# Pair 0 with seven block products in the first layer's two out projections

## The chip, the core and the metric

The kernel runs on one core of a Trainium2 chip. The metric is the device time of one execution in microseconds (us); before the change the median of three runs is 959.14 us (958.94 to 959.21). Five engines work side by side, each through its own instructions in the order in which the program lists them: TensorE (PE in the profile; its weight loads are shown apart as PEld), VectorE (DVE), ScalarE (ACT), GpSimd (POOL) and SyncE (SP), which here issues the DMA transfers. An instruction that needs another engine's result waits for a semaphore, and everything behind it on its engine waits with it.

## The reference, cut to what matters

A decoder trunk of two layers over 256 tokens with 1024 channels. Layer 0 is a short convolution between two half-step FFNs, layer 1 is sparse attention between two such FFNs:

```python
def swiglu_ffn(x, w_in, w_out):
    gate, up = jnp.split(x @ w_in, 2, axis=-1)
    return (jax.nn.silu(gate) * up) @ w_out
...
        h = h + 0.5 * swiglu_ffn(rmsnorm(h, ffn1_norm[i]), ffn1_w_in[i], ffn1_w_out[i])
        hn = rmsnorm(h, mix_norm[i])
        if i < N_A_LAYERS:
            h = h + short_conv_mixer(hn, conv_w_in[i], conv_w[i], conv_w_out[i])
...
        h = h + 0.5 * swiglu_ffn(rmsnorm(h, ffn2_norm[i]), ffn2_w_in[i], ffn2_w_out[i])
```

`w_in` is 1024 x 5632, `w_out` is 2816 x 1024. Everything is float32. The kernel gets near to that precision by splitting each float32 operand into a rounded high part and a remainder, the low part, and multiplying high by high, low by high and high by low.

## The kernel before

**The stages.** For layer 0: FFN 1 (its `ffn_in`, then its out projection `inner_pairs`), the convolution, FFN 2 (the same two steps), then keys and values, the attention layer, and the last FFN. The change touches the two FFNs of layer 0; the program of each is nearly the same.

**`ffn_in`** makes the 2816 hidden channels in 22 tiles of 128, numbered 0 to 21 here. For one tile PE runs 32 matmuls (L487) into a PSUM tile named `mm`. There are two `mm` buffers in use in turn, so a tile's first matmul waits until the tile two before it has been read out. The reading is done in `total`: ACT copies one half out (L505) and DVE adds the other half to it (L506). Then follow, on both engines in turn, the scaling by the norm (L517), silu (L530), gate times up (L531) and the split of the result for the next projection (`Pairs.add`; L499, L500, L554, L555).

**The weights** come through one stream, `W`. SP loads a chunk into a staging buffer (`ws`, of which there are three, or one of a few other places, `W.other`); then for each unit of 1024 columns ACT writes the high part (`high`; L250, or L173 for units of an out projection) and DVE the low part (`low`; L278 or L184) into buffers `wh` and `wl`, six of each. `weave` and `pump` put these two instructions between those of the tile's evacuation, so ACT and DVE carry them in the gaps of the tiles, and some units of the next stage are made while the last tiles of `ffn_in` still run.

**The out projection** takes the hidden tiles two by two: 11 pairs, 0 to 10, with 256 hidden channels each. Tokens, channels and outputs are cut in two, so that a pair is a 2 x 2 by 2 x 2 block product. A pair in `PLAIN0` or `PLAIN1` (the two FFNs) takes eight block products; any other takes seven (a Strassen-like scheme, products 1 to 7) from sums of the operands. Each block product is three matmuls of 128 x 512 (L821). The eight products add up into eight PSUM banks over all pairs: four in banks named `a`, four in two double banks named `mm` (`t57`, which holds products 5 and 7, and `t68`, with 6 and 8). `t57` lies on the buffer that tile 21 of `ffn_in` used, `t68` on that of tile 20. Later PE work in `inner_pairs` turns the sums back into the layout of `h`.

A pair's weights have the units (pair, kind): (p, 0) and (p, 4) for a plain pair; (p, 0), (p, 1), (p, 2) and (p, 3) for a pair with seven products. Kind 1 has half the size and a home of its own (`second_home`). Between kinds 1 and 2 DVE forms sums of the staged weights in place (`sums`, L179: three instructions). On the activation side a plain pair splits both hidden tiles whole; a pair with seven products forms four sums of 128 x 128 (L585) and splits those (L554, L555) when its second tile comes.

`Blocks.product` lists a pair's matmuls in an order that is written out: for a plain pair 0 products 2 and 8, then 4 and 3; for a pair 0 with seven, products 1 and 2, then 6 and 7 together, 5, 3 and 4. `S.ahead` sets how many units may be made before `ffn_in` is over.

Of the kernel before, what the change touches and what calls it, by code (L numbers as in the profile page):

```python
# [10 lines left out]
F32R = mybir.dt.float32r  # L11
# [5 lines left out]
P = 128  # L17
# [22 lines left out]
NBUF = 6  # L40
# [22 lines left out]
def trunk(ctx, tc, A, out):  # L63
# [11 lines left out]
    def mk(shape, tag, bufs, dt=F32, pool=None):  # L75
        uid[0] += 1
        return (pool or sb).tile(list(shape), dt, tag=tag, name=f"{tag}_{uid[0]}", bufs=bufs)
# [10 lines left out]
    def act(shape=(P, 512), dt=F32R):  # L88
        return mk(shape, "act", 22, dt)

    def t2(shape=(P, 512), dt=F32):
        return mk(shape, "t2", 7, dt)
# [19 lines left out]
    class Stream:  # L112
# [9 lines left out]
        def add(self, src, lo=0, hi=None, joint=0):  # L122


            hi = src.shape[1] if hi is None else hi
            while lo < hi:
                n = min(CHUNK, hi - lo)
                for u in range(max(n // 1024, 1)):
                    self.where.append((len(self.src), u, joint))
                self.src.append(src[:, lo:lo + n])  # L130
                lo += n

        def add_pairs(self, src, homes, plain):

            n, c0 = src.shape[1] // CHUNK, len(self.src)
            S = Section()
            S.home, S.plain, S.c0, S.at, S.pair, S.steps = homes, plain, c0, len(self.where), {}, []
            for p in range(n):
                self.paired.add(len(self.src))
                self.src.append(src[:, p * CHUNK:(p + 1) * CHUNK])  # L140
            todo = ([(0, 0), (0, 4)] if 0 in plain else [(0, 0), (0, 1), (0, 2), (0, 3)]) + ([] if 1 in plain else [(1, 0), (1, 1)])
            S.ahead = len(self.where) + len(todo)
            for p in range(n):
                now = [(p + 2, 0), (p + 2, 1)] if p + 2 < n and p + 2 not in plain else []
                if p + 1 < n:
                    last = [(p + 1, 2), (p + 1, 3)]
                    now = [(p + 1, 0), (p + 1, 4)] + now if p + 1 in plain else now + last if p else last + now
                todo += now
                S.steps.append(len(now))
            S.ahead += 3  # L150
            for _ in range(3):
                S.steps[next(p for p in range(n) if S.steps[p])] -= 1
            for p, kind in todo:
                if kind == 1:
                    self.spare.add(len(self.where))
                self.where.append((c0 + p, (S, p, kind), "pair"))
            S.n, S.reach = len(todo), 3
            return S

        def pair_high(self, c, S, p, kind):  # L160
            self.load(c + 2 if p == 0 and kind < 2 else c)
            st = self.stage[c]
            if kind == 1:
                src, (h, l) = st[:, 3:], S.home(p)
            else:
                src = st[:, 2:] if kind in (2, 4) else st[:, :2]
                h, l = mk([P, 2, 512], "wh", NBUF, F32R), None
            if kind == 2 and p > 1:
                self.sums(st)
                for x in range(2):  # L170
                    ac.copy(h[:, x], src[:, x])
            else:
                ac.copy(h, src)  # L173
            self.half.append((src, h, l, st, S, p, kind))

        def sums(self, st):

            for a, b, d, n in ((1, 2, 1, 2), (3, 3, 1, 1), (0, 0, 3, 1)):
                ve.tensor_tensor(out=st[:, a:a + n], in0=st[:, b:b + n], in1=st[:, d:d + n], op=ALU.subtract)  # L179

        def pair_low(self, src, h, l, st, S, p, kind):
            if l is None:
                l = mk([P, 2, 512], "wl", NBUF, F32R)
            ve.tensor_tensor(out=l, in0=src, in1=h.bitcast(F32), op=ALU.subtract)  # L184
            S.pair[p, kind] = h, l
            self.units.append(None)
            if kind == 1 and p < 2:
                self.sums(st)
            if kind in (3, 4):
                self.load(min(S.c0 + p + S.reach, S.c0 + NP + 1))  # L190
# [120 lines left out]

    NP = NF // 2
    PLAIN = (0, 2, 4, 6, 9, 10)
    PLAIN0 = (0, 2, 5, 8, 9, 10)
    PLAIN1 = (0, 2, 5, 8, 9, 10)
    TURNS = (3, 5, 7, 9)

    def second_home(p):
        tag, bufs = ("pr", 6) if p == 0 else ("t2", 7) if p == 1 else ("xs", 8)
        return [mk([P, 1, 512], tag, bufs, F32R) for _ in range(2)]  # L320

    W = Stream()
    W1AT = (13, 13)
    W.add(A["ffn1_w_in"][0])
    SEC0 = W.add_pairs(A["ffn1_w_pairs"], second_home, PLAIN0)
    W.other.update({SEC0.c0 + p: (1, "kt", 0, "ws", "ws")[p % 5] for p in range(NP)})
    SEC0.reach = 4
    W.spare.add(len(W.where) + 2)
    W.add(A["conv_w_in"])
    W.add(A["conv_w_out"])  # L330
    W.add(A["ffn2_w_in"][0])
    SEC1 = W.add_pairs(A["ffn2_w_pairs0"], second_home, PLAIN1)
    W.other.update({SEC1.c0 + p: (1, 0, "ws", "ws", "ws")[p % 5] for p in range(NP)})
    SEC1.reach = 4
    W.spare.add(len(W.where) + 2)
# [14 lines left out]
    W.other.update({n0 + f: (0, 1, "kt", "ws")[f % 4] if f < 14 else ("kt", 0, 1)[(f - 14) % 3] for f in range(4, NF + NP) if f != NF + 2})  # L350
    W.other = {c: at for c, at in W.other.items() if at != "ws"}
    SEC2 = W.add_pairs(A["ffn2_w_pairs1"], second_home, PLAIN)


# [5 lines left out]
    h = [kt8[:, c, :T] for c in range(ND)]  # L360
# [34 lines left out]
    def new_xs():  # L395
        return [mk([P, 512], "xs", 8, F32R) for _ in range(8)]
# [150 lines left out]
    class Pairs:  # L547
# [15 lines left out]
        def add(self, s):  # L563
            self.f.append(s)
            p, odd = divmod(len(self.f) - 1, 2)
            if p in self.plain:
                if not odd:
                    self.left.append([])
                self.left[p] += self.whole(s)
                return  # L570
            if not odd:
                if self.both is None:
                    self.both = act()
                    a = self.both[:, :T]
                else:
                    a, self.both = self.both[:, T:], None
                self.left.append([self.parts(a[:, :P], a[:, P:], s[:, :P])])
                return
            x1, x2 = self.f[-2:]
            a12, a22 = self.whole(x2)  # L580
            self.left[p] += [a12, None, a22]
            t = t2([P, 4, P])
            for o, a, b, op in ((t[:, 0], x1[:, P:], x2[:, P:], ALU.add), (t[:, 1], t[:, 0], x1[:, :P], ALU.subtract),
                                (t[:, 2], x1[:, :P], x1[:, P:], ALU.subtract), (t[:, 3], x2[:, :P], t[:, 1], ALU.subtract)):
                ve.tensor_tensor(out=o, in0=a, in1=b, op=op)  # L585
            h, l = [x.rearrange("p (a m) -> p a m", m=P) for x in self.homes(self.n)]
            self.parts(h, l, t)
            s1, s2, s3, s4 = [(h[:, i], l[:, i]) for i in range(4)]
            self.n += 1
            self.left[p][2] = s4  # L590
            self.left[p] += [s1, s2, s3]
# [109 lines left out]
    xs = new_xs()  # L701
# [89 lines left out]
        return r  # L791

    def first_home(n):
        return [mk([P, 512], "pr", 6, F32R) if x < 6 else mk([P, 512], "hm", 5, F32R) for x in (2 * n, 2 * n + 1)]

    X = {}

# [32 lines left out]
    def inner_pairs(S, left, rows, make, hold, first):  # L830
# [12 lines left out]
        def plus(name, n, tt):  # L843
            add(s[name], n, s[name], tt)
# [12 lines left out]
        def firsts():  # L857
            s["s1"], s["u2"], s["u3"] = t2(), t2(), t2()
            ac.copy(s["s1"], m[1])
            add(s["u2"], 6, s["s1"])  # L860
            add(s["u3"], 7, s["u2"])
# [58 lines left out]

    W.cap = SEC0.ahead
    hid = Pairs(first_home, PLAIN0)
    ffn_in(xs, nm, sums=first_tiles(), rms=first_rms, hid=hid, bg=rows_bg)

# [63 lines left out]

    inner_pairs(SEC0, hid.left, X["rows"], conv_norm, t2, conv_first)
    del hid  # L990
    xs, nm = X["xs"], X["nm"]
# [21 lines left out]
    xs = new_xs()  # L1013
# [29 lines left out]

    W.cap = SEC1.ahead
    hid = Pairs(first_home, PLAIN1)
    ffn_in(xs, nm, pre=lambda: list(tab), bg=second_bg, hid=hid)

# [101 lines left out]

    inner_pairs(SEC1, hid.left, X["rows"], lambda: nm, lambda: mk([P, 512], "pr", 6), kv_first)  # L1150
    del hid
    xs = new_xs()
# [167 lines left out]
    xs = new_xs()  # L1320
# [320 lines left out]
    xs = new_xs()  # L1641
# [189 lines left out]
```

## Time and profile before

| what | value |
|---|---|
| runs | 958.94, 959.14, 959.21 us |
| profiled execution, its own time | 959.4 us |
| its span, first to last instruction | 957.5 us |
| mean granted TensorE clock | 1.000 |
| PE busy / DVE busy / ACT busy | 99% / 84% / 64% of the span |
| `ffn_in` of FFN 1, tiles 3 to 21 | 24.78 to 130.37 us |
| matmuls of its out projection begin | 130.37 us |
| the same in FFN 2 | 400.79 us |

The rows of the timeline give the start in us from the first instruction, the duration in us, the engine, the line, the operation, the tiles written and read, shapes and a count of merged instructions; in brackets the idle time of the engine ahead of it and what ended it. The chain of waits follows the last instruction back to what released it. Ends of matmuls are modelled (one of 128 x 512 shows 0.39 us while its successor starts 0.23 us after it), so the distance from start to start is what counts on PE; on DVE an instruction may start some 0.08 us before the one ahead of it ends, and there too the distance between starts is used.

### The profile page before, as it was taken

Reading aid. Unit: us, or ns where it says so; the run is one execution under the profiler, and the core shown is the slowest. Engines: PE = TensorE matmul, PEld = TensorE weight load, DVE = VectorE, ACT = ScalarE, POOL = GpSimd, SP = SyncE. Lnnn points to the kernel's source line nnn. Section 1 sums busy time; section 2 is a strip of 40 time slices with the busy share of each in tenths; the row PEclk is TensorE's granted clock in tenths of the full one; section 3 lists DMA queues with packets and bytes.
Section 4 is the critical chain, followed back from the end, with each engine's and each line's share of the span. In section 5 each row is a group of like instructions: output and inputs, shape, how many; then the busy total and the mean of one; then the engine's idle time right before and its main releaser. Section 6 shows DMA issues by size and latency. Waiting matters only on the chain.

```text
span 957.5 us, 14525 instructions
## 1 busy us (share of the span) xinstructions
PE 951.2 (99%) x5431; PEld 827.5 (86%) x5431; DVE 803.5 (84%) x1332; ACT 613.0 (64%) x1048; POOL 144.5 (15%) x231
## 2 busy tenths in 40 slices
PE   8999999999999999999999999999999999999998
PEld 7888888888888888888888898889987888888887
DVE  6898899898898888898969787866588888878996
ACT  7666565565556666565857777754579656656553
POOL 1000000024460000000021042001337350000002
PEclk9999999999999999999999999999999999999999
DMA  8665844364546567553636867554520363467452
GB/s 300 230 216 186 307 149 160 132 208 164 201 138 243 197 208 254 175 196 132 220 132 188 265 212 259 177 201 163 215 89 2 132 221 143 166 222 247 148 179 84
DMA packets 42150, 178.58 MB, mean 187 GB/s; under 512 B 3777, under 2 KB 7505, under 8 KB 27105
## 3 DMA queue, kind: packets, MB, share of 16 engines
q1 hardware_dynamic: 42080, 177.67, 54.1%
q8 instruction: 42, 0.69, 0.3%
q14 instruction: 28, 0.22, 0.1%
HBM read 175.52 MB, written 1.08 MB: 184 GB/s over the span
## 4 chain that ended last, share of the span: by engine, by line
PE 97%; DVE 1%; ACT 1%; DMA 1%; SPq 0%; issue 0%
PE mm L487 55%; PE a L487 13%; PE a L821 12%; PE mm L821 5%; PE a L1124 1%; PE mm L1477 1%; PE a L1547 1%; PE mm L728 1%; PE a L1522 1%; PE a L767 1%; DMA base<-in_first_dram 1%; DVE pr L1485 0%; PE a L1217 0%; PE a L1063 0%; PE a L1065 0%; PE a L1064 0%
## 5 line engine op out<-in xcount | busy, mean ns | idle before, releaser
L487 PE MATMUL mm<-xs,wh 128*128 128x512 f32 x1480 | 349.2, 390 | 0.0
L487 PEld LDWEIGHTS mm<-xs,wh 128*128 128x128 f32 x1480 | 273.6, 188 | 54.8 <-DVE xs L410 0.5
L278 DVE TENSOR_TENSOR wl<-ws,wh 128x1024 fp32r<-128x1024 f32 x217 | 271.1, 1258 | 28.2 <-ACT wh L250 18.4
L250 ACT CAST wh<-ws 128x1024 fp32r<-128x1024 f32 x217 | 224.6, 1045 | 14.9 <-PE a L487 7.3
L487 PEld LDWEIGHTS mm<-xs,wl 128*128 128x128 f32 x1480 | 185.2, 192 | 4.2
L487 PE MATMUL mm<-xs,wl 128*128 128x256 f32 x1480 | 187.3, 283 | 0.0
L506 DVE TENSOR_TENSOR t<-mm,t 128x512 f32<-128x512 f32 x95 | 65.2, 686 | 46.2 <-ACT t L505 45.5
L505 ACT COPY t<-mm 128x512 f32<-128x512 f32 x95 | 55.4, 583 | 52.5 <-PE mm L487 51.8
L821 PE MATMUL a<-wh,act 128*128 128x512 f32 x306 | 81.7, 390 | 0.0
L821 PEld LDWEIGHTS a<-wh,act 128*128 128x128 f32 x306 | 57.3, 188 | 11.8
L530 ACT ACTIVATE t<-t 128x256 f32<-128x256 f32 x88 | 36.8, 418 | 45.9 <-DVE t L517 45.7
L487 PE MATMUL a<-act,wh 128*128 128x512 f32 x256 | 60.0, 390 | 0.0
L487 PEld LDWEIGHTS a<-act,wh 128*128 128x128 f32 x256 | 47.5, 188 | 9.4
L499 ACT CAST act<-t 128x256 fp32r<-128x256 f32 x81 | 33.0, 407 | 29.1 <-DVE t L944 18.5
L406 ACT ACTIVATE xs<-base 128x256 fp32r<-128x256 f32 x32 | 16.1, 508 | 50.1 <-DVE base L637 35.2
L517 DVE TENSOR_TENSOR t<-t,R 128x256 f32<-128x256 f32 (+1 forms) x88 | 45.0, 511 | 2.6
L821 PE MATMUL a<-wl,act 128*128 128x512 f32 x153 | 46.9, 389 | 0.0
L184 DVE TENSOR_TENSOR wl<-base,wh 128x1024 fp32r<-128x1024 f32 x38 | 45.6, 1221 | 0.1
L531 DVE TENSOR_TENSOR t<-t,t 128x256 f32<-128x256 f32 x88 | 37.0, 420 | 4.1 <-ACT t L530 4.1
L500 DVE TENSOR_TENSOR act<-t,act 128x256 fp32r<-128x256 f32 x81 | 35.5, 438 | 4.7 <-ACT act L499 4.7
L173 ACT CAST wh<-base 128x1024 fp32r<-128x1024 f32 x33 | 33.6, 1045 | 4.8 <-DVE base L179 3.0
L821 PEld LDWEIGHTS a<-wl,act 128*128 128x128 f32 x153 | 28.7, 188 | 6.0
(361 smaller groups left out, 1405.5 us busy)
## 6 DMA issues: line engine op xcount, KB each, us to landing
ws<-in_ffn_w_in_dram SPq DMA_DIRECT2D x69, 1024.0 KB, 4.9
base<-in_ffn_w_pairs_dram SPq DMA_DIRECT2D x32, 512.0 KB, 4.8
ws<-in_conv_w_in_dram SPq DMA_DIRECT2D x12, 1024.0 KB, 4.8
ws<-in_ffn_w_pairs_dram SPq DMA_DIRECT2D x22, 512.0 KB, 4.9
ws<-in_ffn_w_out_dram SPq DMA_DIRECT2D x11, 1024.0 KB, 4.8
base<-in_ffn_w_in_dram SPq DMA_DIRECT2D x11, 1024.0 KB, 5.3
kt<-in_ffn_w_pairs_dram SPq DMA_DIRECT2D x12, 512.0 KB, 4.5
ws<-in_w_kv_dram SPq DMA_DIRECT2D x6, 1024.0 KB, 4.9
```

What stands on the lines that cost most here:

```text
L173: ac.copy(h, src)
L184: ve.tensor_tensor(out=l, in0=src, in1=h.bitcast(F32), op=ALU.subtract)
L250: ac.copy(h, src)
L278: ve.tensor_tensor(out=l, in0=src, in1=h.bitcast(F32), op=ALU.subtract)
L487: pe.matmul(o if x == 0 else o[:, :T], u[x][:, q * P:(q + 1) * P], rhs if x == 0 else rhs[:, :T], start=start, stop=stop, skip_group_check ...
L500: ve.tensor_tensor(out=dst[:, T:], in0=src, in1=dst[:, :T].bitcast(F32), op=ALU.subtract)
L505: ac.copy(r, o[:, :, T:])
L506: ve.tensor_tensor(out=r, in0=o[:, :, :T], in1=r, op=ALU.add)
L517: ve.tensor_tensor(out=r, in0=r, in1=R[:, None, :].to_broadcast([P, n, T]), op=ALU.mult)
L530: ac.activation(s, r[:, 0], AF.Silu)
L531: ve.tensor_tensor(out=s, in0=s, in1=r[:, 1], op=ALU.mult)
L821: pe.matmul(self.m[n], x, w, start=(c == 0), stop=(c == 3 * self.total[n] - 1), skip_group_check=True)
```

## The change

It has four parts.

1. `PLAIN0` and `PLAIN1` lose pair 0, so that six of the eleven pairs take seven products in both FFNs of layer 0. `PLAIN`, of the last FFN, keeps it.
2. The first unit (0, 0) of such a section no longer takes a buffer of `wh` and one of `wl`: it has its own place, the tile `kt` (`own`). The home of (0, 1) is in `act` instead of `pr`. Since `kt` is taken, the staging places of the first section become those of the second, (kt8, kt8, ws, ws, ws).
3. Pair 0's sums of the weights come at its kind 1, those of pair 1 now at kind 2 like the later ones. The half unit (p + 2, 1) is made after (p + 1, 2) and (p + 1, 3) instead of ahead of them.
4. The sums of pair 0's activations are formed when the sixth hidden tile (tile 5) is added, not when its second is. The new method is `sums`.

```diff
-        def add_pairs(self, src, homes, plain):
+        def add_pairs(self, src, homes, plain, own=()):
...
-                    now = [(p + 1, 0), (p + 1, 4)] + now if p + 1 in plain else now + last if p else last + now
+                    now = [(p + 1, 0), (p + 1, 4)] + now if p + 1 in plain else now[:1] + last + now[1:] if p else last + now
...
-                if kind == 1:
+                if kind == 1 or (p, kind) in own:
                     self.spare.add(len(self.where))
...
-                h, l = mk([P, 2, 512], "wh", NBUF, F32R), None
-            if kind == 2 and p > 1:
+                if (p, kind) in S.own:
+                    t = mk([P, 4, 512], "kt", 1, F32R)
+                    h, l = t[:, :2], t[:, 2:]
+                else:
+                    h, l = mk([P, 2, 512], "wh", NBUF, F32R), None
+            if kind == 2 and p > (0 in S.plain):
...
-            if kind == 1 and p < 2:
+            if kind == 1 and p <= (0 in S.plain):
                 self.sums(st)
...
-    PLAIN0 = (0, 2, 5, 8, 9, 10)
-    PLAIN1 = (0, 2, 5, 8, 9, 10)
+    PLAIN0 = (2, 5, 8, 9, 10)
+    PLAIN1 = (2, 5, 8, 9, 10)
...
-        tag, bufs = ("pr", 6) if p == 0 else ("t2", 7) if p == 1 else ("xs", 8)
+        tag, bufs = ("act", 22) if p == 0 else ("t2", 7) if p == 1 else ("xs", 8)
...
-    SEC0 = W.add_pairs(A["ffn1_w_pairs"], second_home, PLAIN0)
-    W.other.update({SEC0.c0 + p: (1, "kt", 0, "ws", "ws")[p % 5] for p in range(NP)})
+    SEC0 = W.add_pairs(A["ffn1_w_pairs"], second_home, PLAIN0, [(0, 0)])
+    W.other.update({SEC0.c0 + p: (1, 0, "ws", "ws", "ws")[p % 5] for p in range(NP)})
...
+                if len(self.f) == 6 and 0 not in self.plain:
+                    self.sums(0)
                 return
...
-            x1, x2 = self.f[-2:]
-            a12, a22 = self.whole(x2)
+            a12, a22 = self.whole(s)
             self.left[p] += [a12, None, a22]
+            if p:
+                self.sums(p)
+
+        def sums(self, p):
+            x1, x2 = self.f[2 * p:2 * p + 2]
             t = t2([P, 4, P])
```

**The end of `ffn_in` on DVE.** This is DVE in FFN 1 between tile 18 and tile 19 of `ffn_in` (`act_212` and `act_214` hold tile 18's split, `mm_222` and `mm_227` are tile 19). Before:

```order
L500 TENSOR_TENSOR act_212_1196<-t1_209_1187,act_212_1196 128x256
L506 TENSOR_TENSOR t2_214_1232<-mm_213_1199,t2_214_1232 128x512
L517 TENSOR_TENSOR t2_214_1232<-t2_214_1232,R_47_310 128x256
L278 TENSOR_TENSOR wl_216_1238<-ws_202_1139,wh_215_1236 128x1024
L531 TENSOR_TENSOR t1_217_1240<-t1_217_1240,t2_214_1232 128x256
L278 TENSOR_TENSOR wl_220_1248<-ws_202_1139,wh_218_1243 128x1024
L500 TENSOR_TENSOR act_221_1250<-t1_217_1240,act_221_1250 128x256
L506 TENSOR_TENSOR t2_223_1286<-mm_222_1253,t2_223_1286 128x512
L517 TENSOR_TENSOR t2_223_1286<-t2_223_1286,R_47_310 128x256
L184 TENSOR_TENSOR wl_225_1294<-base_70,wh_224_1292 128x1024
```

and now, from the split of the same tile 18:

```order
L505 TENSOR_TENSOR act_222_1257<-t1_219_1248,act_222_1257 128x256
L189 TENSOR_TENSOR kt_224_1263<-base_70,kt_224_1263 128x1024
L189 TENSOR_TENSOR act_226_1267<-base_70,act_225_1266 128x512
L184 TENSOR_TENSOR base_70<-base_70 128x2x512
L184 TENSOR_TENSOR base_70<-base_70 128x512 x2
L511 TENSOR_TENSOR t2_228_1306<-mm_227_1273,t2_228_1306 128x512
L522 TENSOR_TENSOR t2_228_1306<-t2_228_1306,R_47_310 128x256
L189 TENSOR_TENSOR wl_230_1312<-base_70,wh_229_1310 128x1024
```

Between tile 18's split and tile 19's reading stand five instructions that were not there: the low parts of (0, 0) and (0, 1) and the three weight sums of pair 0. In the tile's own places for units stand (0, 2) and (0, 3) where (0, 0) and (0, 4) stood. In FFN 2 the same five stand at the same place.

**The start of the out projection on PE.** These are the first rows on PE behind tile 21 in FFN 1, with the semaphores that each waits for. `act_59`, `act_61` and `pr` are pair 0's activations. Before (`mm_255` is `t68`; `t57` is not written by pair 0, its first row is pair 1's):

```order
L821 MATMUL a_251_1424<-wh_224_1292,act_61_346 128x512 x2
L821 MATMUL a_251_1424<-wl_225_1294,act_59_339 128x512 [waits DVE_49]
L821 MATMUL a_251_1424<-wl_225_1294,act_61_346 128x512
L821 MATMUL mm_255_1428<-wh_227_1299,act_59_339 128x512 [waits DVE_49]
L821 MATMUL mm_255_1428<-wh_227_1299,act_59_339 128x512
L821 MATMUL mm_255_1428<-wh_227_1299,act_61_346 128x512 x2
```

and now (`mm_260` is `t68`, `mm_259` is `t57`):

```order
L832 MATMUL a_255_1442<-kt_224_1263,act_59_339 128x512 x2
L832 MATMUL a_256_1443<-kt_224_1263,act_61_346 128x512 x2
L832 MATMUL a_255_1442<-kt_224_1263,act_59_339 128x512
L832 MATMUL a_256_1443<-kt_224_1263,act_61_346 128x512
L832 MATMUL mm_260_1447<-wh_229_1310,pr_94_528 128x512 [waits DVE_49]
L832 MATMUL mm_260_1447<-wh_229_1310,pr_95_529 128x512
L832 MATMUL mm_259_1446<-wh_229_1310,pr_94_528 128x512 [waits DVE_49]
L832 MATMUL mm_259_1446<-wh_229_1310,pr_95_529 128x512
```

The first write into `t57` moves from the 34th matmul of the section (pair 1's tenth) to the ninth. In the built program that row waits for DVE's addition of tile 21, the last reader of the buffer; the first write into `t68` waits for that of tile 20.

**The sixth tile on DVE.** This is DVE in FFN 1 behind the split of the sixth hidden tile (`act_92`, `act_93`). Before, the reading of the next tile follows at once:

```order
L500 TENSOR_TENSOR act_93_521<-t1_89_512,act_93_521 128x256
L506 TENSOR_TENSOR t2_95_557<-mm_94_524,t2_95_557 128x512
L517 TENSOR_TENSOR t2_95_557<-t2_95_557,R_47_310 128x256
L278 TENSOR_TENSOR wl_97_563<-ws_77_448,wh_96_561 128x1024
L531 TENSOR_TENSOR t1_98_565<-t1_98_565,t2_95_557 128x256
```

and now:

```order
L505 TENSOR_TENSOR act_92_520<-t1_88_511,act_92_520 128x256
L596 TENSOR_TENSOR t2_93_523<-t1_55_330,t1_60_343 128x128
L596 TENSOR_TENSOR t2_93_523<-t2_93_523,t1_55_330 128x128
L596 TENSOR_TENSOR t2_93_523<-t1_55_330 128x128
L596 TENSOR_TENSOR t2_93_523<-t1_60_343,t2_93_523 128x128
L560 TENSOR_TENSOR pr_95_529<-t2_93_523,pr_94_528 128x512
L511 TENSOR_TENSOR t2_97_565<-mm_96_532,t2_97_565 128x512
```

Five instructions now stand ahead of tile 6's reading, the last of them behind ACT's copy of the sums.

More of the change, by code (lines that the diff above doesn't have):

```diff
@@ L137, in add_pairs @@
             S.home, S.plain, S.c0, S.at, S.pair, S.steps = homes, plain, c0, len(self.where), {}, []
+            S.own = own
             for p in range(n):
@@ L331, in trunk @@
     W.add(A["ffn2_w_in"][0])
-    SEC1 = W.add_pairs(A["ffn2_w_pairs0"], second_home, PLAIN1)
+    SEC1 = W.add_pairs(A["ffn2_w_pairs0"], second_home, PLAIN1, [(0, 0)])
     W.other.update({SEC1.c0 + p: (1, 0, "ws", "ws", "ws")[p % 5] for p in range(NP)})
@@ L793, in first_home @@
     def first_home(n):
-        return [mk([P, 512], "pr", 6, F32R) if x < 6 else mk([P, 512], "hm", 5, F32R) for x in (2 * n, 2 * n + 1)]
+        return [mk([P, 512], "pr", 6, F32R) if x < 6 else mk([P, 512], "hm", 5, F32R) if x < 11 else act() for x in (2 * n, 2 * n + 1)]
     X = {}
```

## The prediction

> **What bounds the kernel now.** The page comes first: shares of busy time, and the chain of work that ended last.
>
> ```profile
> span 957.5 us, 14525 instructions
> PE 951.2 (99%) x5431; PEld 827.5 (86%) x5431; DVE 803.5 (84%) x1332; ACT 613.0 (64%) x1048; POOL 144.5 (15%) x231
> ...
> PE 97%; DVE 1%; ACT 1%; DMA 1%; SPq 0%; issue 0%
> ```
>
> TensorE works 951.2 of 957.5 us, and 97% of the chain lies on it. The view of PE's waits shows how little is lost; these are the two largest of its four rows, and all four sum to 3.0 us:
>
> ```profile
> PE mm L728 <- ACT wh L719: 1.4, 2, 1.1
> PE a L376 <- DVE ones L356: 1.1, 1, 1.1
> ```
>
> None of them stands in a section that the change touches. So a matmul taken out is worth its full pitch, and there is no wait here that could shrink. What can go wrong is a new wait: VectorE is busy 84% over all, and the change gives it more to do at the end of `ffn_in`, so the question is how long PE can go on there without it.
>
> **What the change removes.** Pair 0 takes seven block products, not eight: three matmuls of 128 x 512 fewer in each of two sections. Their pitch stands in the chain of waits:
>
> ```profile
> 131.90 1.36 PE mm L821 x6
> ...
> 133.26 4.76 PE a L821 x21
> ```
>
> 4.76 / 21 = 0.2267 us, and 1.36 / 6 gives the same. Six matmuls are **1.36 us**, 0.14% of the run. This is all that the change can gain.
>
> **What it adds on DVE ahead of tile 19.** FFN 1's section begins on PE at 130.37. These are the rows of DVE before it, and the start of the section on PE:
>
> ```profile
> 118.23 0.42 DVE L500 TENSOR_TENSOR act<-t,act 128x256 fp32r<-128x256 f32 x1
> 120.08 0.69 DVE L506 TENSOR_TENSOR t<-mm,t 128x512 f32<-128x512 f32 x1 [1.43 <-ACT t L505]
> ...
> 125.62 0.69 DVE L506 TENSOR_TENSOR t<-mm,t 128x512 f32<-128x512 f32 x1 [1.40 <-ACT t L505]
> 126.34 0.42 DVE L517 TENSOR_TENSOR t<-t,R 128x256 f32<-128x256 f32 x1
> 126.69 1.22 DVE L184 TENSOR_TENSOR wl<-kt,wh 128x1024 fp32r<-128x1024 f32 x1
> 127.82 0.42 DVE L531 TENSOR_TENSOR t<-t,t 128x256 f32<-128x256 f32 x1
> 128.16 0.69 DVE L184 TENSOR_TENSOR t<-kt,t 128x512 fp32r<-128x512 f32 x1
> 128.76 2.67 DVE L179 TENSOR_TENSOR kt<-kt 128x1024 f32<-128x1024 f32 x3
> 131.35 0.42 DVE L500 TENSOR_TENSOR act<-t,act 128x256 fp32r<-128x256 f32 x1
> 131.88 1.23 DVE L184 TENSOR_TENSOR wl<-kt,wh 128x1024 fp32r<-128x1024 f32 x1
> 133.02 0.68 DVE L506 TENSOR_TENSOR t<-mm,t 128x512 f32<-128x512 f32 x1
> ```
>
> ```profile
> 130.37 1.07 PE L821 MATMUL a<-wh,act 128*128 128x512 f32 x4
> 131.28 0.61 PE L821 MATMUL a<-wl,act 128*128 128x512 f32 x2
> 131.73 1.07 PE L821 MATMUL mm<-wh,act 128*128 128x512 f32 x4
> ...
> 137.85 1.07 PE L821 MATMUL mm<-wh,pr 128*128 128x512 f32 x4
> ```
>
> The five inserted instructions have counterparts here, from start to start: a full low part 126.69 to 127.82, 1.13; a half one 128.16 to 128.76, 0.60; the three weight sums 128.76 to 131.35, 2.59. Together **4.32 us**, behind tile 18's split at 118.23. The two old units (0, 0) and (0, 4) are replaced one for one by (0, 2) and (0, 3).
>
> Then the lateness is followed tile by tile. Ahead of tile 19's reading (120.08) DVE idled for 1.43, and since an instruction may start 0.08 before the one ahead ends, 1.51 can be filled: 4.32 - 1.51 = 2.81 late. Ahead of tile 20's (125.62) it idled 1.40, or 1.48: 1.33 late. Between tile 20 and 21 there is no idle row; only the step from the split at 131.35 to the low part at 131.88 takes 0.53, where 0.34 is usual (126.34 to 126.69, for a tile of the same shape), because it waits for ACT's copy of the summed weights. That copy is now made in two halves, each behind its own sum, and I take 0.13 of the 0.19 as gained. Tile 21's addition is **1.20 late**: it starts at 134.22 and, with 0.68, ends at 134.90.
>
> Before, nobody waited for that. Pair 0 wrote no product into `t57`, whose buffer tile 21 has just left; the first to do so was the 34th matmul, at 137.85, 4.15 after the old end at 133.70. (The write into `mm` at 131.73, ahead of tile 21's addition at 133.02, is `t68`, on tile 20's buffer.) Now the ninth matmul writes `t57`. It is due eight pitches into the section, 130.37 + 1.81 = 132.18. Even with DVE as early as before it would wait 133.70 - 132.18 = 1.52. With DVE late, **134.90 - 132.18 = 2.72 us** of hold on PE, and PE's queue has nothing that can pass it.
>
> FFN 2 has the same gaps and times:
>
> ```profile
> 390.50 0.69 DVE L506 TENSOR_TENSOR t<-mm,t 128x512 f32<-128x512 f32 x1 [1.44 <-ACT t L505]
> ...
> 396.04 0.69 DVE L506 TENSOR_TENSOR t<-mm,t 128x512 f32<-128x512 f32 x1 [1.40 <-ACT t L505]
> ...
> 403.44 0.68 DVE L506 TENSOR_TENSOR t<-mm,t 128x512 f32<-128x512 f32 x1
> ```
>
> ```profile
> 400.79 1.07 PE L821 MATMUL a<-wh,act 128*128 128x512 f32 x4
> ```
>
> 403.44 + 0.68 + 1.20 = 405.32 against 400.79 + 1.81 = 402.60: again **2.72**.
>
> The bounds of one hold are 1.52 (DVE no later than before) and 133.70 + 4.32 - 132.18 = 5.84 (no gap absorbs anything). I take 2.72, since the two gaps are measured rows and what ends them, ACT's copy of a finished tile, waits only for PE; DVE fills such gaps in order.
>
> **The activation sums at the sixth tile.** Pair 1's, which stand in the trace, show what such a block takes from its first sum to the tile's next row, with the wait for ACT's high part inside; behind them the split that shrinks, and tile 6's reading:
>
> ```profile
> 37.33 0.28 DVE L555 TENSOR_TENSOR act<-t,act 128x128 fp32r<-128x128 f32 x1
> ...
> 41.45 0.61 DVE L585 TENSOR_TENSOR t<-t,t 128x128 f32<-128x128 f32 x2
> ...
> 43.77 0.42 DVE L517 TENSOR_TENSOR t<-t,R 128x256 f32<-128x256 f32 x1
> ...
> 50.11 0.69 DVE L506 TENSOR_TENSOR t<-mm,t 128x512 f32<-128x512 f32 x1
> ```
>
> ```profile
> 48.93 7.44 PE L487 MATMUL mm<-xs,wh 128*128 128x512 f32 x32
> ```
>
> 43.77 - 41.45 = 2.32 us, now ahead of tile 6's reading at 50.11. Pair 0's first tile is split only in half (0.28, where a whole one is 0.42 as at 118.23), so 0.14 goes. The reading would end at 50.11 + 0.69 + 2.32 - 0.14 = 52.98. The 32 merged rows on PE are tile 7's last sixteen and tile 8's first sixteen; (7.44 - 0.16) / 32 = 0.2275 is their pitch, with 0.16 for the last one's modelled tail (0.39 against 0.23). Tile 8 takes the buffer that tile 6 leaves, at 48.93 + 16 x 0.2275 = 52.57. That is a hold of **0.41 us**, where 1.77 was to spare; its bounds are 0, if DVE regains that much in tiles 4 and 5, and 2.32 - 1.77 = 0.55. In FFN 2 PE stands otherwise to DVE at this tile:
>
> ```profile
> 318.81 0.68 DVE L506 TENSOR_TENSOR t<-mm,t 128x512 f32<-128x512 f32 x1
> ```
>
> ```profile
> 319.35 7.44 PE L487 MATMUL mm<-xs,wh 128*128 128x512 f32 x32
> ```
>
> The reading ended at 319.49, and PE needs the buffer at 319.35 + 3.64 = 322.99. The 3.50 between cover 2.32: no hold.
>
> **What is costed at nothing.** Moving the half units behind (p + 1, 2) and (p + 1, 3), and pair 1's sums from kind 1 to kind 2, changes only the order on ACT and DVE within a section, where they run ahead of PE:
>
> ```profile
> 164.79 2.46 DVE L184 TENSOR_TENSOR wl<-base,wh 128x1024 fp32r<-128x1024 f32 x2
> ...
> 178.85 0.75 DVE L841 SCALAR_TENSOR_TENSOR t<-a,sm,t 128x512 f32<-128x512 f32 x1 [2.07 <-PE a L821]
> ```
>
> ```profile
> 168.00 0.61 PE L821 MATMUL mm<-wl,hm 128*128 128x512 f32 x2
> ```
>
> The first unit of the two merged at 164.79 ends at 166.01, and PE uses it at 168.00: 1.99 in hand. DVE enters the section 1.20 late but PE 2.72, so the cover grows. At the section's end it is DVE that waits for PE (2.07), so PE's lateness is not caught up: the same work follows it. The cost if the cover went would be what DVE is late beyond 1.99.
>
> SP's order changes too: with `kt` taken, staging of FFN 1's pairs goes to `ws`, and the first chunk of the convolution is held until pair 7's is used. FFN 2 already stages so, and its successor there is the case to read:
>
> ```profile
> 437.70 22.32 SPq L209 DMA_DIRECT2D ws<-in_w_kv_dram  x5
> 444.95 2.01 ACT L250 CAST wh<-ws 128x1024 fp32r<-128x1024 f32 x2
> ```
>
> The first of those loads is issued 7.25 ahead of the copy that needs it, and no row of PE waits there; so nothing is charged.
>
> **The sum.** Against the profiled execution's 959.4: 959.4 - 1.36 + 0.41 + 2.72 + 2.72 = 963.9. The profiled execution lies 0.26 above the median of the runs, 959.14, so the forecast is **963.6 us**, 0.5% slower.
>
> **The clock.** A hold of 2.72 is longer than any in the trace. The longest is the 1.1 us at L728; two windows show PE's granted clock (third figure from the end) while it waits there and behind it:
>
> ```profile
> 6.00:8.00 2.00, 0.86 (x6) 0.60 (x5) 0.73 (x2) 1.27 (x4) 0.00 (x0) 1.00 1.00 387
> 8.00:10.00 2.00, 2.00 (x10) 1.62 (x11) 1.53 (x6) 2.00 (x7) 0.00 (x0) 1.00 1.03 424
> ```
>
> PE works 0.86 of the first 2.00 us, and the clock is 1.00 in both, so I charge nothing. [...]
>
> **The rivals.**
>
> *No hold.* If tile 21's last addition were over by 132.18, the saving would stand alone: 959.14 - 1.36 = 957.8. It decides from the point where DVE has regained all it was given and 1.52 more. For it: no idle row stands ahead of the addition, so only DVE's own queue holds it. Against it: DVE carries 4.32 more there. 9%. That the products do not really go is excluded by the changed order on PE, which has six matmuls fewer.
>
> *A short hold.* If DVE absorbs all it is given, by gaps in other places (ACT's copy earlier, pair 0's shorter split), each hold is 1.52: 959.14 - 1.36 + 0.41 + 3.04 = 961.2, or 960.8 without the tile-six hold. For it: DVE idles 16% over all. Against it: between tile 20's reading and tile 21's there is no idle row. 14%.
>
> *Lateness that nothing absorbs.* DVE's queue is in order: if the low parts wait for ACT, or the weight sums for their staged chunks, the gaps ahead of tiles 19 and 20 fill with waiting, and the hold goes towards 5.84: half a gap in each section gives 965.1, all of them 959.14 - 1.36 + 0.41 + 11.68 = 969.9. For it: ACT is late with tile 19's split when DVE is. Against it: ACT too has nothing to do in those gaps but wait for PE. 8%.
>
> *A drop of the clock.* If PE's clock halved behind each hold for as long as the hold lasted, twelve matmuls would take double the pitch, 12 x 0.2267 = 2.72 more in each section: 963.6 + 5.4 = 969.0. For it: a stop of this length stands nowhere in the trace, so nothing excludes it. Against it: the stop of 1.1 us leaves the clock at 1.00. 4%.
>
> The forecast, from 962.5 to 965, keeps 65%. The no-hold rival is the one on the other side.
>
> **How the numbers follow.** The range goes from 960.8 (short holds, no tile-six hold) to 966.0 (half of one gap not absorbed in both sections, and a little more); it leaves out the no-hold case and most of the two long ones, 18%. About 0.2% (1.9 us) is what a measurement of this kernel can tell from no change. Slower by more than that is anything above 961.06: the forecast, both long rivals and half of the short one, 0.85. Within it lie the other half of the short holds and most of the no-hold case, which at -1.36 is itself within 0.2%: 0.13. Faster keeps 0.02.
>
> **What would show it.** In the profile after: PE with 5425 matmuls and clock 1.00; in PE's waits one row of the out projection on `mm`, two times, about 2.7 us each, ended by DVE's addition of tile 21; a row of about 0.4 at tile 8 of FFN 1; on DVE no idle time ahead of tiles 19 and 20, and tile 21's addition 1.2 us after its old place. Wrong would be: no wait at the ninth matmul (then the buffers lie otherwise than I read), idle time on DVE between its low parts and sums (then the lateness is mis-sized), or a wait of PE later in the section (then the cover I counted on is not there).

## The result and the profile after

Six runs of the changed kernel have a median of 965.42 us (964.94 to 967.85), beside 959.09 us (958.80 to 959.92) for six of the kernel before: a ratio of 1.0070, 95% interval 1.0057 to 1.0083. It is slower by 6.3 us, where 4.5 had been forecast (963.6, within 960.8 to 966.0).

The page of the changed kernel, its size, its busy engines and the engines of the chain:

```profile
span 963.2 us, 14547 instructions
...
PE 952.1 (99%) x5425; PEld 827.1 (86%) x5425; DVE 815.6 (85%) x1352; ACT 618.1 (64%) x1056; POOL 144.6 (15%) x231
...
PE 88%; DVE 8%; ACT 2%; issue 1%; DMA 1%; SPq 0%
```

Six matmuls are gone, PE's busy time is none the less 0.9 us longer, and the chain, 97% on PE before, now passes through DVE for 8% of the span. PE's waits on others name the places (engine, line, what it waited for: us in all, times, longest):

```profile
PE mm L832 <- DVE t L511: 5.1, 2, 2.6
...
PE mm L492 <- DVE t L511: 0.4, 1, 0.4
```

Neither row was there before. PE's timeline has the two long ones, each at the ninth matmul of its section, the first write into `t57`:

```profile
130.12 1.52 PE L832 MATMUL a<-kt,act 128*128 128x512 f32 x6
131.48 0.61 PE L832 MATMUL mm<-wh,pr 128*128 128x512 f32 x2
134.66 0.74 PE L832 MATMUL mm<-wh,pr 128*128 128x512 f32 x2 [2.57 <-DVE t L511]
135.23 0.62 PE L832 MATMUL mm<-wl,pr 128*128 128x512 f32 x2
```

```profile
402.82 1.52 PE L832 MATMUL a<-kt,act 128*128 128x512 f32 x6
404.18 0.61 PE L832 MATMUL mm<-wh,pr 128*128 128x512 f32 x2
407.36 1.22 PE L832 MATMUL mm<-wh,pr 128*128 128x512 f32 x2 [2.57 <-DVE t L511]
408.38 1.05 PE L832 MATMUL mm<-wl,pr 128*128 128x512 f32 x2
```

Counted from the start due (eight pitches, 1.81, behind the section's start) both holds are 2.73 us: 134.66 - 131.93 and 407.36 - 404.63. Idle shows 0.16 less, since the end of the matmul ahead is modelled. What follows is not the same. After the first hold two matmuls take 0.57 (134.66 to 135.23), near the usual 0.45; after the second the same two take 1.02. The granted clock, third figure from the end of these windows, says why:

```profile
134.66:136.00 1.34, 1.34 (x6) 1.12 (x7) 1.34 (x2) 0.90 (x2) 0.00 (x0) 1.00 0.53 101
```

```profile
404.60:407.36 2.76, 0.19 (x2) 0.00 (x1) 2.69 (x5) 2.23 (x4) 0.00 (x0) 0.95 0.00 0
407.36:408.40 1.04, 1.04 (x3) 0.85 (x4) 1.04 (x2) 0.60 (x2) 0.00 (x0) 0.50 0.63 71
409.40:410.40 1.00, 1.00 (x4) 0.81 (x3) 1.00 (x2) 1.00 (x2) 0.00 (x0) 0.50 0.66 141
410.40:411.40 1.00, 1.00 (x5) 0.77 (x5) 1.00 (x3) 0.65 (x2) 0.00 (x0) 0.96 0.80 254
```

Behind the first hold the granted clock is 1.00. In the second it falls to 0.50 just before PE starts again (407.07 against 407.36), and stays there until about 410.5.

DVE before the first section, from the inserted low part to tile 21's addition:

```profile
118.31 1.22 DVE L189 TENSOR_TENSOR kt<-base,kt 128x1024 fp32r<-128x1024 f32 x1
119.44 0.68 DVE L189 TENSOR_TENSOR act<-base,act 128x512 fp32r<-128x512 f32 x1
120.04 2.67 DVE L184 TENSOR_TENSOR base<-base 128x1024 f32<-128x1024 f32 x3
122.63 0.68 DVE L511 TENSOR_TENSOR t<-mm,t 128x512 f32<-128x512 f32 x1
...
126.68 0.69 DVE L511 TENSOR_TENSOR t<-mm,t 128x512 f32<-128x512 f32 x1
...
133.92 0.68 DVE L511 TENSOR_TENSOR t<-mm,t 128x512 f32<-128x512 f32 x1
```

The five inserted instructions take 122.63 - 118.31 = 4.32 us, and neither gap ahead of tiles 19 and 20 has an idle time any more. Tile 21's addition ends at 134.60, and PE starts 0.06 later.

### The profile page after: what moved, and what is told of

It reads as the page before. It is cut to its first block, busy times and chain, and to the rows that moved or that the text cites. A ratio compares the mean times of both kernels' runs of the same rounds, so it can differ in the third digit from the quotient of the medians.

```text
span 963.2 us, 14547 instructions
## 1 busy us (share of the span) xinstructions
PE 952.1 (99%) x5425; PEld 827.1 (86%) x5425; DVE 815.6 (85%) x1352; ACT 618.1 (64%) x1056; POOL 144.6 (15%) x231
## 4 chain that ended last, share of the span: by engine, by line
PE 88%; DVE 8%; ACT 2%; issue 1%; DMA 1%; SPq 0%
PE mm L492 49%; PE a L492 13%; PE a L832 11%; PE mm L832 6%; DVE wl L283 2%; PE a L1135 1%; DVE base L184 1%; PE mm L1488 1%; DMA base<-in_first_dram 1%; DVE wl L189 1%; PE a L1558 1%; DVE t L511 1%; PE a L1533 1%; DVE t L536 0%; DVE pr L1496 0%
## 5 line engine op out<-in xcount | busy, mean ns | idle before, releaser
L283 DVE TENSOR_TENSOR wl<-ws,wh 128x1024 fp32r<-128x1024 f32 x217 | 271.4, 1260 | 29.6 <-ACT wh L255 19.8
L832 PE MATMUL a<-wh,act 128*128 128x512 f32 x286 | 76.8, 390 | 0.0
L832 PEld LDWEIGHTS a<-wh,act 128*128 128x128 f32 x286 | 53.8, 189 | 11.1
L832 PE MATMUL a<-wl,act 128*128 128x512 f32 x143 | 44.0, 389 | 0.0
L189 DVE TENSOR_TENSOR wl<-ws,wh 128x1024 fp32r<-128x1024 f32 x32 | 38.2, 1221 | 0.2 <-ACT wh L178 0.2
```

The costliest lines, as they stand in the source:

```text
L832: pe.matmul(self.m[n], x, w, start=(c == 0), stop=(c == 3 * self.total[n] - 1), skip_group_check=True)
```

## Where the 6 us are

Four rows give the length of each section up to the next stage, the last two of them of the kernel before:

```profile
190.00 1.18 PE L492 MATMUL mm<-xs,wh 128*128 128x512 f32 x4
...
464.16 0.71 PE L1135 MATMUL a<-wh,kt 128*128 128x512 f32 x2
```

```profile
188.08 1.18 PE L487 MATMUL mm<-xs,wh 128*128 128x512 f32 x4
...
458.49 0.71 PE L1124 MATMUL a<-wh,kt 128*128 128x512 f32 x2
```

FFN 1's section took 188.08 - 130.37 = 57.71 and now 190.00 - 130.12 = 59.88: 2.17 more, which is -0.68 (three matmuls), +2.73 (the hold) and +0.12 (the first two matmuls behind it). FFN 2's took 57.70 and now 61.34: 3.64 more, the same two terms and 1.59 for the slow start at half clock. With 0.67 at tile 8 of FFN 1 (below), 6.5 us are accounted for, against 6.3 between the medians. (The two spans differ by 5.7 only: the profiled execution of before spent 0.7 us more on its waits at the very start, 1.4 beside 0.7 at the same statement. Those waits read 0.2 to 0.8 in the profiles of the experiments, and nothing in two of them.)

## The experiments

Each is an edit of the changed kernel unless it says otherwise, timed beside the kernel before on the same chip.

**The order of pair 0's products.** Nothing changes but which matmuls of pair 0 come first:

```diff
+            if p == 0 and p not in S.plain:
+                for n in (3, 6, 4, 7, 5):
+                    B.product(p, n)
             B.product(p, *(8, 4, 3) if p in S.plain else (3, 7, 6, 5, 4) if 0 < p < last else (1, 6, 7, 5, 2, 3, 4))
```

> The changed kernel, but pair 0's products in both sections of layer 0 run 1, 2, 3, 6, 4, 7, 5 one after another, so that the first write into t57 is the 16th matmul and not the 9th; the same matmuls, nothing changed on DVE. Theory (PE's lost time is the wait of t57 for tile 21's addition): that addition still ends about 4.5 us into the section, the write is due at 15 x 0.2267 = 3.40, so each hold shrinks from 2.73 (from the start due to the start found) by 7 x 0.2267 = 1.59 to about 1.1 us. Clock: if the half clock seen behind FFN 2's hold comes from the length of the stop, it is 1.00 everywhere now. Time then 965.4 - 2 x 1.59 - about 1.6 to 2 = 960.3 to 960.7; without an effect on the clock 962.2. Rival (DVE's load itself delays PE, wherever the products stand): 965 to 966, with a hold of the old length at another row.

Measured: 960.51 us, ratio 1.0015 (1.0006 to 1.0024), mean clock 0.999 or more in all ten executions. The first section on PE:

```profile
130.00 1.52 PE L832 MATMUL a<-kt,act 128*128 128x512 f32 x6
...
134.54 0.73 PE L832 MATMUL mm<-wh,pr 128*128 128x512 f32 x2 [0.98 <-DVE t L511]
```

Due at 130.00 + 3.40 = 133.40, started at 134.54: 1.14, in FFN 2 alike. The wait moved with the product, and shrank by the seven pitches by which its first write moved back. With 965.42 - 960.51 = 4.9 saved against 3.2 from the two holds, the half clock is gone as well.

**No hold at all.** Products 7 and 5 of pair 0 go behind pair 1's first two, and the activation sums behind tile 6's reading:

```diff
             B.product(p, *(2, 4 if p else 8) if p in S.plain else (1, 2))
+            if p == 1:
+                B.product(0, 7)
+                B.product(0, 5)
             B.prepare(p)
+            if p == 0 and p not in S.plain:
+                for n in (3, 6, 4):
+                    B.product(p, n)
+                continue
...
-                if len(self.f) == 6 and 0 not in self.plain:
-                    self.sums(0)
...
             sums.append(total2(o) if f == n0 and n0 else total(o, 2))
+            if isinstance(hid, Pairs) and len(hid.f) == 6 and len(sums) == 1 and 0 not in hid.plain:
+                hid.sums(0)
```

> The changed kernel, but (a) pair 0's products 7 and 5, the only ones on t57, come behind pair 1's products 1 and 2 (the 22nd matmul, due at 21 x 0.2267 = 4.76 us into the section, behind the addition's end at 4.5), and (b) pair 0's activation sums stand behind tile 6's reading, not ahead of it. DVE's and ACT's work is the same in amount. Theory: no hold in either section, none at tile 8 of FFN 1, clock 1.00 throughout; only the six matmuls are left: 959.1 - 1.36 = 957.7, 0.14% below the kernel before. Rival (DVE's 4.3 us more per section show up later, in a late unit of pair 1 or 2 or at the end of the section): 959 to 962, with a new wait of PE in the section.

Measured: 957.51 us, ratio 0.9983 (0.9974 to 0.9992). All of PE's waits on others:

```profile
PE a L381 <- DVE ones L361: 1.1, 1, 1.1
PE mm L739 <- ACT wh L730: 0.7, 2, 0.5
PE a L1546 <- DVE xs L1550: 0.3, 1, 0.3
PE a L1540 <- POOL pr L1532: 0.2, 1, 0.2
```

None is in the sections. The work added on DVE is all still there (815.4 us busy, beside 815.6), so here the load alone costs nothing that can be seen: its place ahead of a reading that PE waited for did. The experiment above changes the order alone, the next one the place of the sums alone. This version beats both kernels, by 1.6 us and 7.9 us.

**The activation sums alone.** Only the second half of that edit, the sums behind tile 6's reading:

> The changed kernel, but pair 0's activation sums stand behind tile 6's reading, not ahead of it; the rest as changed. Theory: PE's short wait at tile 8 of FFN 1 (0.37 idle, start 0.54 late) goes, and nothing comes in its place, since from tile 6 to 7 DVE takes 3.9 us where PE takes 5.5: 965.4 - 0.5 to 0.7 = 964.8, the holds at t57 unchanged at 2.7. Rival: DVE is late all the same and the wait stands at tile 9: no change, 965.4. The clock may fall behind none, one or both of the holds (1.6 us each), which blurs the time; the trace decides.

Measured: 964.69 us, ratio 1.0053 (1.0040 to 1.0067). At tile 8 the changed kernel has these rows:

```profile
48.00 3.81 PE L492 MATMUL mm<-xs,wh 128*128 128x512 f32 x16
52.18 3.93 PE L492 MATMUL mm<-xs,wh 128*128 128x512 f32 x16 [0.37 <-DVE t L511]
55.95 2.32 PE L492 MATMUL mm<-xs,wl 128*128 128x256 f32 x18
```

and this experiment one without a break:

```profile
48.13 7.44 PE L492 MATMUL mm<-xs,wh 128*128 128x512 f32 x32
55.41 4.00 PE L492 MATMUL mm<-xs,wl 128*128 128x256 f32 x32
```

From 48.00 to 55.95 are 7.95 us, from 48.13 to 55.41 7.28: the wait is worth 0.67, of which 0.54 is the late start and the rest the slower first matmuls behind it. The medians differ by 0.73, which would not settle it alone, since the clock moves the executions of both kernels by more; the rows do. The four executions are 962.89, 964.38, 964.99 and 965.79, at mean clocks of 1.000, 0.998, 0.998 and 0.996. By an estimate from the profiled execution of the changed kernel, with 3.41 us at 0.50 and a mean of 0.998, that fits a clock that fell behind none, one or both of the holds.

**A longer hold.** One more low part on DVE ahead of tile 21's addition:

```diff
-            ve.tensor_tensor(out=l, in0=src, in1=h.bitcast(F32), op=ALU.subtract)
+            for _ in range(2 if (p, kind) == (1, 2) and 0 not in S.plain else 1):
+                ve.tensor_tensor(out=l, in0=src, in1=h.bitcast(F32), op=ALU.subtract)
```

> The changed kernel with one more full low part on DVE (unit (1, 2) subtracted twice, 1.13 us) ahead of tile 21's addition, in both sections. Theory: nothing absorbs it, each hold grows from 2.73 to 3.86. Time from the holds alone 965.4 + 2.3 = 967.7. [...] Rival (DVE makes up for it before the addition): 965.4.

Measured: 970.69 us, ratio 1.0116 (1.0102 to 1.0129), 3.0 more than the 967.7 from the holds alone. PE's row for the place reads

```profile
PE mm L833 <- DVE t L512: 7.7, 2, 3.8
```

so each hold grew by 1.26 (3.83 idle at both places), a little more than the added 1.13. Mean clocks were 0.993 to 0.996 in all four executions, and both sections of the profiled one have the half clock. In the first it begins only after PE has started again (135.94):

```profile
135.70:136.00 0.30, 0.06 (x1) 0.06 (x1) 0.27 (x2) 0.00 (x0) 0.00 (x0) 1.00 0.00 0
136.00:136.30 0.30, 0.30 (x2) 0.25 (x3) 0.30 (x2) 0.00 (x0) 0.00 (x0) 0.92 0.00 0
...
139.30:139.60 0.30, 0.30 (x2) 0.30 (x1) 0.30 (x2) 0.05 (x1) 0.00 (x0) 0.50 0.76 253
139.60:139.90 0.30, 0.30 (x2) 0.19 (x2) 0.30 (x1) 0.30 (x1) 0.00 (x0) 0.89 0.96 348
```

A window of 0.30 us with a mean of 0.92 was at half for 16% of it, so the fall is at 136.25 and, in the same way, the return at 139.67: 3.42 us. The profiled execution (969.29 us, clock 0.996) is the fastest of the four. One such piece takes 0.5 x 3.41 / 968 = 0.0018 off the mean clock, so by this estimate the two executions at 0.993 had about four pieces, not two; no profile shows where the others lay.

**A hold of 1.8 us.** As the first experiment, with the order 3, 6, 7, 5, 4:

> The changed kernel, but pair 0's products run 1, 2, 3, 6, 7, 5, 4 one after another: the first write into t57 is the 13th matmul, due at 12 x 0.2267 = 2.72 us into the section, so each hold should measure 4.5 - 2.72 = 1.8 from the start due (about 1.65 shown as idle). [...] A stop of 1.65 leaves at least 51% of any such stretch busy: clock 1.00 in every execution, time 965.4 - 2 x 0.9 - 1.6 to 2 (the clock) = 961.6 to 962. Rival (any stop above about 1 us can bring the half clock): mean clock 0.998 or less in some executions, 963.5.

Measured: 961.88 us, ratio 1.0032 (1.0021 to 1.0044); idle 1.66 at both places, mean clock 0.999 or more in all six executions. In FFN 1:

```profile
134.59 0.73 PE L832 MATMUL mm<-wh,pr 128*128 128x512 f32 x2 [1.66 <-DVE t L511]
```

```profile
134.59:138.00 3.41, 3.41 (x15) 2.83 (x16) 3.41 (x6) 2.86 (x5) 0.00 (x0) 1.00 0.75 177
```

A stop of 1.66 did not bring the half clock in any of these twelve cases, and one of 2.57 did in some of those above. The 51% of the expectation is (3.4 - 1.65) / 3.4, for a stretch as long as the half clock lasted in the changed kernel's FFN 2 (3.41, from 407.07 to 410.48). That PE's share of work in such a stretch decides was the author's estimate; no run shows it.

**A hold of 5 us.** The longer hold with two low parts more, not one:

> The changed kernel with two more full low parts on DVE (2.27 us) ahead of tile 21's addition in both sections: holds of 2.73 + 2.27 = 5.0. Theory: half clock behind (or from within) both holds in every execution, but for no longer than before, since only what is left of a 3.4 us stretch when PE starts again costs time: 965.4 + 4.5 + 0 to 1.6 = 970 to 972, mean clock 0.996 or less. Rival (the half clock lasts as long as the stop did): 5 us at half pace behind each hold, 5.0 lost in all, above 973.

Measured: 972.86 us, ratio 1.0148 (1.0131 to 1.0164), between the two ranges. PE stood idle from 132.55 to 137.63 in FFN 1:

```profile
134.50:134.80 0.30, 0.00 (x0) 0.00 (x0) 0.30 (x1) 0.13 (x1) 0.00 (x0) 1.00 0.00 0
134.80:135.10 0.30, 0.00 (x0) 0.00 (x0) 0.30 (x1) 0.00 (x0) 0.00 (x0) 0.74 0.00 0
...
141.40:141.70 0.30, 0.30 (x3) 0.20 (x2) 0.30 (x1) 0.21 (x1) 0.00 (x0) 0.50 0.99 369
141.70:142.00 0.30, 0.30 (x3) 0.26 (x2) 0.30 (x1) 0.30 (x1) 0.00 (x0) 0.88 1.00 389
```

Half clock from 134.94 to 141.77, 6.83 us or twice 3.41, with PE at work for the last 4.1 of them. The expectation had one such stretch behind each hold; here the first has two.

**FFN 1 alone.** Pair 0 of FFN 2 plain again:

```diff
-    PLAIN1 = (2, 5, 8, 9, 10)
+    PLAIN1 = (0, 2, 5, 8, 9, 10)
...
-    SEC1 = W.add_pairs(A["ffn2_w_pairs0"], second_home, PLAIN1, [(0, 0)])
+    SEC1 = W.add_pairs(A["ffn2_w_pairs0"], second_home, PLAIN1)
```

> The changed kernel with pair 0 of FFN 2 plain again (eight products there, no place of its own, sums at the old place); FFN 1 as changed. Theory: the costs of the two FFNs add up. FFN 1 alone: -0.68 for three matmuls, +0.5 to 0.7 at tile 8, +2.7 to 2.85 for its hold: 959.1 + 2.6 = 961.7, or 963.3 where the half clock follows. Rival (most of the loss is one common cause, such as the staging of the weights): 959 or 965.

Measured: 963.36 us, ratio 1.0048 (1.0033 to 1.0063), so 4.3 more than the kernel before, with a mean clock of 0.998 in all four executions. The half clock here stands behind FFN 1's hold, where the profiled execution of the changed kernel had none:

```profile
135.15 0.73 PE L832 MATMUL mm<-wh,pr 128*128 128x512 f32 x2 [2.57 <-DVE t L511]
135.73 0.92 PE L832 MATMUL mm<-wl,pr 128*128 128x512 f32 x2
136.45 1.05 PE L832 MATMUL mm<-wh,pr 128*128 128x512 f32 x2
```

The section takes 61.51 us up to the next stage (130.61 to 192.12), 3.80 more than in the kernel before: -0.68 + 2.73 + 0.12, and 1.63 for the half clock. With 0.67 at tile 8 that is 4.5, against 4.3 between the medians: the costs are each section's own, and FFN 1's hold is no safer from the clock than FFN 2's.

**Staging and homes alone.** Pair 0 plain in both FFNs, with the place of its own, the homes, the staging places and the order of the half units as changed:

```diff
-    PLAIN0 = (2, 5, 8, 9, 10)
-    PLAIN1 = (2, 5, 8, 9, 10)
+    PLAIN0 = (0, 2, 5, 8, 9, 10)
+    PLAIN1 = (0, 2, 5, 8, 9, 10)
```

> The changed kernel with pair 0 plain in both FFNs of layer 0: all products as before, but with the place of its own for unit (0, 0), the other homes and staging places and the new order of the half units. Theory (these parts cost nothing): 959.1, within 0.4, and PE's waits those of before. Rival (the later load of the convolution's first chunk or the later half units cost something that the holds hid): 960 to 962, with a wait of PE in or behind FFN 1's section.

Measured: 958.56 us, ratio 0.9997 (0.9988 to 1.0007), with no wait of PE that the kernel before did not have. The median is 0.5 lower than that of the kernel before (959.06), a little more than the 0.4 allowed for, and the interval takes in no difference at all: these parts cost nothing that was measured.

## Why the prediction was right, and where it fell short

The median, 965.42, lies within the stated range of 960.8 to 966.0, and above the 962.5 to 965 that had been given 65%.

- **Six matmuls, -1.36.** Right: the version without holds is 1.56 below the kernel before (957.51 to 959.07), with an interval of 0.8 to 2.5.
- **The lateness of DVE, 1.20.** Right. Against PE's start of the section the addition began 133.02 - 130.37 = 2.65 into it and now 133.92 - 130.12 = 3.80: 1.15 later. The inserted work took the 4.32 that had been put together from other rows, and the way down was as reckoned: tile 19's reading was 2.80 late (2.81 forecast), tile 20's 1.31 (1.33), and from there to tile 21's DVE took 7.24, not 7.40, a gain of 0.16 (0.13).
- **The hold at the ninth matmul, 2.72 in each section.** Right, 2.73 twice. That it agrees to 0.01 is luck: the addition ended 0.05 earlier than forecast against PE, and PE starts 0.06 after its end, which no term held. The first experiment shows that the wait belongs to the bank, as it goes back with the product.
- **The sums at the sixth tile, 0.41.** Right in place and mechanism, too small: 0.67. Of the 0.14 taken off for the shorter split only 0.06 was left at tile 6's reading, and PE started 0.05 after the reading's end, so the start is 0.54 late, near the upper bound of 0.55. The matmuls that begin again after the wait take 0.13 longer, which no term held; two behind FFN 1's long hold take 0.12 longer (0.57, where 0.45 is usual).
- **No hold in FFN 2 at this tile, nothing for staging and homes, no catching up later.** Right: the waits view has one such row only, the staging kernel is not told from the one before, and the sections end later by what they lost.
- **The clock, nothing charged.** This step failed. It took a stop of 1.1 us that left the clock alone as a sign for one of 2.7, and gave the drop 4%, behind both holds or neither. By an estimate from their mean clocks four of the six executions had one piece of half clock (0.998) and two had two (0.996), though only one of them has a profile. In that one the piece cost 1.5 us beside the slower restart, and with FFN 1 alone 1.6: the largest part of the 1.8 us by which the forecast fell short. No run shows the term of that rival, half pace for as long as each hold lasted: in the profile one hold of 2.73 had none of it behind it, and with the other the clock was at 0.50 for 3.41 us, 0.29 of them before PE started again. Neither the forecast nor that rival was the outcome, but a mixture: 963.6 + 0.26 (tile 8) + 0.24 (two restarts) + 1.5 (one drop) = 965.6, where 965.42 was measured.

## What to carry to other kernels

Where work is taken off a saturated engine, look at which of its results is now asked for first: here the seven products cost less than eight, but one of them wrote a bank whose last reader stood at the end of a queue without idle time, and 0.7 us saved became 2.7 us of waiting until the other products went ahead of it. The sum of the load on the helping engine did not tell this; the distance between one reading and the first write behind it did. And the length of a stop on TensorE need not be its whole price: here one of 2.7 us cost some 1.5 to 1.6 more when the clock fell to 0.50 (FFN 2 of the changed kernel, FFN 1 alone).

## What the hardware showed

In every profile with a half clock (0.50) it lasted 3.41 or 3.42 us, or twice that: 3.42 and 6.83 in the windows above, 3.41 in FFN 2 of the changed kernel (407.07 to 410.48), and 3.41 here, in the profile of FFN 1 alone, from 135.87 to 139.28:

```profile
135.70:136.00 0.30, 0.30 (x2) 0.19 (x1) 0.30 (x1) 0.30 (x2) 0.00 (x0) 0.78 0.84 123
136.00:136.30 0.30, 0.30 (x2) 0.28 (x1) 0.30 (x1) 0.30 (x2) 0.00 (x0) 0.50 0.59 137
139.00:139.30 0.30, 0.30 (x2) 0.29 (x1) 0.30 (x1) 0.30 (x1) 0.00 (x0) 0.53 0.91 355
139.30:139.60 0.30, 0.30 (x2) 0.22 (x2) 0.30 (x2) 0.30 (x2) 0.00 (x0) 1.00 1.02 396
```

In these profiles it began at no fixed distance from the stop: inside it (2.3 us after PE's last matmul in FFN 2 of the changed kernel), or 0.3 (the longer hold) and 0.7 us (FFN 1 alone) after PE had started again. Two profiles have a fall in both sections. These are FFN 2's, with the longer hold and with the hold of 5 us:

```profile
412.60:412.90 0.30, 0.30 (x3) 0.20 (x2) 0.30 (x1) 0.30 (x1) 0.00 (x0) 0.72 0.70 212
```

```profile
414.80:415.10 0.30, 0.27 (x1) 0.27 (x2) 0.28 (x1) 0.00 (x0) 0.00 (x0) 0.56 0.00 0
```

They give falls at 412.73 and 414.84, where PE had started again at 411.54 and 414.83: 1.19 and 0.01 us behind the start.

In the 3.41 us ahead of these falls PE had worked at most 35% of the time: in the changed kernel 33% (1.13 of 3.41: its last matmul ended at 404.79, and the row below puts the fall at 407.07), with FFN 1 alone 25%, and 35% where the longer hold fell in FFN 2.

```profile
406.80:407.10 0.30, 0.00 (x0) 0.00 (x0) 0.30 (x1) 0.07 (x1) 0.00 (x0) 0.95 0.00 0
```

FFN 1's hold in the changed kernel shows the other side. The stop there lasted from 132.09 to 134.66, and the clock stayed at 1.00, though in the 3.41 us ahead of PE's new start it had worked only 25% of the time:

```profile
131.25:134.66 3.41, 0.84 (x5) 0.38 (x3) 3.31 (x6) 2.67 (x4) 0.00 (x0) 1.00 0.00 0
```

So a share as low as this did not always bring the half clock. Where the stop is 1.66, PE worked at least (3.41 - 1.66) / 3.41 = 51% of any 3.41 us, and none of six executions fell (mean clock 0.999 or more). What decides between the two outcomes of a stop of 2.57 was not shown by these runs.
